# Moving the low parts of split weights 64 bytes off the grid of the other operands

## Chip, cores and metric

The kernel runs on one core of a Trainium2 chip. The time is in device microseconds for one execution; lower is better.

## What is computed

Two layers of a hybrid block on 256 tokens of width 1024, all in float32. Each layer has a SwiGLU feed-forward network, a mixer (a gated short convolution, a gated linear recurrence and a multi-scale pooling side by side), cross-attention to a memory of 256 tokens, and a second SwiGLU network, each followed by a layer norm:

```python
def reference(x, mem, ...):
    h = x
    for l in range(DEPTH):                                   # DEPTH = 2
        h = layer_norm(ALPHA * h + 0.5 * swiglu(h, ffn1_gate[l], ffn1_up[l], ffn1_down[l]), ...)
        z = h @ w_in[l]
        cb, cc, ch, rq, rf, ri, rg, pu = jnp.split(z, split_at, axis=-1)
        y_conv = short_gated_conv(ch, cb, cc, conv_w[l])
        y_rec = hgrn2(rq, rf, ri, rg, lbs[l], rec_norm_g[l])
        y_pool = multiscale_pool(pu, pool_w[l], pool_scale[l])
        mix = jnp.concatenate([y_conv, y_rec, y_pool], axis=-1) @ w_out[l]
        h = layer_norm(ALPHA * h + mix, ...)
        h = layer_norm(ALPHA * h + cross_attn(h, mem, ca_q[l], ca_k[l], ca_v[l], ca_o[l]), ...)
        h = layer_norm(ALPHA * h + 0.5 * swiglu(h, ffn2_gate[l], ffn2_up[l], ffn2_down[l]), ...)
    return h
```

Nearly all the work is in the products with the weights (1024 x 2816, 1024 x 1024 and the like), which are read once from HBM.

## The kernel before

Every large product is made in three passes of the type float32r. Each operand is split into a high part, its value rounded to float32r, and a low part, the rest. The product is then high x high + high x low + low x high. Weights come in slabs: `load` (line 62) issues a DMA of 1 MB into a tile `raw` of 128 partitions x 2048, and splits it in halves of 128 x 1024. `split` (line 58) is two instructions: ScalarE copies `raw` to `whi` (line 59), and VectorE subtracts that from `raw` into `wlo` (line 60). `raw` has 3 buffers, `whi` and `wlo` have 8 each. The activations are kept transposed and split as well: `xT` (and `mT` for the memory) holds for each of 8 blocks of 128 channels 256 columns of high parts and, right behind them, 256 of low parts.

Two helpers make the products:

- `mm_cols` (line 94) makes 128 output columns for all tokens. The weight block is the stationary operand. Seven products of the high part with 512 columns of `x`, high and low side by side (line 97), eight of the low part with the 256 high columns (line 99), and the last of the high part (line 100).
- `mm_rows` (line 108) makes 512 output columns for 128 tokens. The activation is stationary and the weights stream past it: line 109 high by high, line 110 the low weights, line 111 the low activations with the high weights.

TensorE's weight load of a matmul is a record of its own in the profile (PEld) and runs beside the matmul before it. The order of the work is the order of the program on each engine's queue; the tile framework places the waits, from the tiles and their numbers of buffers.

What the change is about is where tiles lie in SBUF. Each partition has its memory filled pool after pool, in the order in which the pools are opened, and in a pool tag after tag. The framework's constants and the small tiles `prm`, `invc`, `lbs`, `oml` and `nhalf` (padded to 16 columns) fill the first 512 bytes, so that all that follows begins on a multiple of 512: `h`, the unit matrices, `xT`, `mT`, `kTh`, `kTl`, `rows`, `wpool` and `masks` (896 bytes used of a tile of 1024) in the pool `cst`; then `raw`, `whi`, `wlo` and the layer norm's `lng` and `lnb` in the pool `wp`; then the pool `sm` of small statistics, and behind it the pools of the stages (`ffn`, `mix`, `att`), which share one place. In the mixer's pool some tiles at the end don't begin on such a multiple: `cv`, `win` and `u` begin 320 bytes past one. `masks` holds, as bytes, which pairs of positions belong to each of 7 levels of the recurrence. GpSimd makes it once (line 201), and line 597 reads it in slices of 64 bytes.

Of the kernel before, what the change touches and what calls it, by code (L numbers as in the profile page):

```python
# [8 lines left out]
F32 = mybir.dt.float32  # L9
F32R = mybir.dt.float32r  # L10
U8 = mybir.dt.uint8
# [6 lines left out]
P = 128  # L18
DEPTH = 2
SEQ = 256  # L20
DM = 1024
DFF = 2816
NT = SEQ // P
# [6 lines left out]
LEVELS = (1, 2, 4, 8, 16, 32, 64)  # L30
# [16 lines left out]
def model(ctx: ExitStack, tc: tile.TileContext, t: dict, out: bass.AP):  # L47
    nc = tc.nc
    cst = ctx.enter_context(tc.tile_pool(name="cst", bufs=1))
    wp = ctx.enter_context(tc.tile_pool(name="wp", bufs=1))  # L50
    sm = ctx.enter_context(tc.tile_pool(name="sm", bufs=2))
    ps = ctx.enter_context(tc.tile_pool(name="ps", bufs=4, space=PSUM))

# [4 lines left out]
    def split(hi, lo, src):  # L58
        nc.scalar.copy(hi, src)  # L59
        nc.vector.tensor_tensor(lo, src, hi.bitcast(F32), op=ALU.subtract)  # L60

    def load(src, k0, nk, c0, ncol, fine=False):


        hi, lo, todo = [], [], []
        step = 2048 // ncol
        for a in range(k0, k0 + nk, step):
            raw = wp.tile([P, 2048], F32, tag="raw", name="raw", bufs=3)
            raw = raw.rearrange("p (k c) -> p k c", c=ncol)
            half = step // 2  # L70
            part = 1 if fine else step
            for b in range(0, step, part):
                nc.sync.dma_start(
                    raw[:, b : b + part, :],
                    src[(a + b) * P : (a + b + part) * P, c0 : c0 + ncol].rearrange("(k p) c -> p k c", p=P),
                )
            for s in range(2):
                h = wp.tile([P, 1024], F32R, tag="whi", name="whi", bufs=8)
                w = wp.tile([P, 1024], F32R, tag="wlo", name="wlo", bufs=8)
                h = h.rearrange("p (k c) -> p k c", c=ncol)  # L80
                w = w.rearrange("p (k c) -> p k c", c=ncol)
                r = raw[:, s * half : (s + 1) * half, :]
                if fine:
                    todo += [(h[:, b, :], w[:, b, :], r[:, b, :]) for b in range(half)]
                else:
                    split(h, w, r)
                hi.append(h)
                lo.append(w)
        return Weights(hi, lo, half, todo)
# [23 lines left out]
    def tok(i):  # L113
        return slice(i * P, (i + 1) * P)
# [6 lines left out]
    oml = cst.tile([P, DEPTH, HEADS], F32, name="oml")  # L121
    nhalf = cst.tile([P, 16], F32, name="nhalf")[:, 0:HEADS]
    h = [cst.tile([P, DM], F32, name=f"h{i}") for i in range(NT)]
    for i in range(NT):
        for n in range(2):
            c = slice(n * 512, n * 512 + 512)
            nc.sync.dma_start(h[i][:, c], t["x"][0, tok(i), c])
# [24 lines left out]
    def load_memory(mp):  # L152
# [10 lines left out]

    rows = cst.tile([P, P], F32, name="rows")
    wpool = cst.tile([P, DEPTH, 2, P], F32, name="wpool")
    masks = cst.tile([P, 1024], U8, name="masks")[:, 0 : NT * len(LEVELS) * 64].rearrange(
        "p (b n c) -> p b n c", b=NT, c=64
    )
    nc.gpsimd.memset(nhalf, -0.5)
    cw = prm[:, 0:12].rearrange("p (l k j) -> p l k j", l=DEPTH, j=2)  # L170
    ng = prm[:, 20:28].rearrange("p (l h) -> p l h", l=DEPTH)
# [66 lines left out]


    def ln_params(l, n):  # L240
        g = wp.tile([P, DM], F32, tag="lng", name="lng")
        b = wp.tile([P, DM], F32, tag="lnb", name="lnb")
        nc.sync.dma_start(g, t["ln_g"][l, n : n + 1, :].to_broadcast([P, DM]))
        nc.sync.dma_start(b, t["ln_b"][l, n : n + 1, :].to_broadcast([P, DM]))
        return g, b
# [83 lines left out]
    def ffn(l, name, n, pend=None, last=False, early=None):  # L329
        gate, up, down = (t[f"{name}_{x}"][l] for x in ("gate", "up", "down"))  # L330
        with tc.tile_pool(name="ffn", bufs=2, reuse_waits="tile") as fp:
# [7 lines left out]
            def first():  # L339

                ah, al = act_tiles()
                wg = load(gate, 0, NK, 0, CHUNK, fine=pend is None)
                wu = load(up, 0, NK, 0, CHUNK) if pend is not None else None

                def products(o, w, i, k):
# [15 lines left out]
                if pend is None:  # L361
# [5 lines left out]
                    with tc.manual_schedule(engines={E.Activation, E.DVE, E.PE}):  # L367
# [5 lines left out]
                        for a in range(0, NK, 2):  # L373
                            for k in range(a + 4, min(a + 6, NK)):
                                split(*wg.todo[k])
                            group(0, wg, a)
                    wu = load(up, 0, NK, 0, CHUNK)
                    for a in range(0, NK, 2):
                        group(1, wu, a)
# [64 lines left out]
            for c, (c0, ncol) in enumerate(chunks):  # L444
                if c:
                    acts.append(hidden(c0, ncol, late))
                    late = None
                else:
                    a, late = first()
                    acts.append(a)  # L450
                    ys = [[acc((P, 512), "dn") for _ in range(2)] for _ in range(NT)]
                if c == 1:
                    gb = ln_params(l, n)
                if c == 1 and early is not None:
                    rest = early(fp)
                if c == 2 and early is not None:
                    for f in rest:
                        f()
                if c > 0:
                    if c > 1:  # L460
                        both(c - 2, 1)
                    if c < len(chunks) - 1:
                        both(c - 1, 0)
# [38 lines left out]
    def mixer(l, fill):  # L502
        w_in = t["w_in"][l]
        with tc.tile_pool(name="mix", bufs=1, reuse_waits="tile") as mp:
# [31 lines left out]
            columns(1280, 512, lambda j, o: add(f[:, :, j, :], o, by_tile), ev_f)  # L536
            columns(768, 512, lambda j, o: add(q[:, :, j, :], o, by_tile))
            gb = ln_params(l, 1)
            w = load(w_in, 0, NK, 1792, 512)
            for i in range(NT):  # L540
# [171 lines left out]
    def attention(l, pend):  # L712
        scale = (DM // HEADS) ** -0.5
        with tc.tile_pool(name="att", bufs=1, reuse_waits="tile") as ap:
# [62 lines left out]
            values(l, 0, vh, vl, {6: pend})  # L777
            query(0)
            gb = ln_params(l, 2)
            query(1, lambda: (weights(0), weights(1)))  # L780
            values(
# [48 lines left out]
```

## Time and profile before

| | |
|---|---|
| median of 3 runs | 1174.87 us (1174.75 to 1176.64) |
| the profiled execution | 1176.58 us, of it 1174.8 us span of instructions |
| granted TensorE clock | 0.998 |
| TensorE busy, matmuls | 1161.9 us (99%) |
| TensorE busy, weight loads | 1001.2 us (85%) |
| VectorE busy | 824.7 us (70%) |
| ScalarE busy | 595.6 us (51%) |
| DMA | 218.23 MB, 186 GB/s on average |

A busy share is the part of the span in which the engine had an instruction under way. For matmuls it counts overlapping ones once, and their ends are modelled, so starts are the better guide to their pace. "PE" is the matmuls, "PEld" the weight loads, DVE is VectorE, ACT is ScalarE. The chain that ended last is followed back from the last instruction, at each step to what released it.

### The profile page before, as it was taken

How to read it: one execution, taken by the hardware profiler on the slowest of the kernel's cores; microseconds unless marked ns; L12 is line 12 of the kernel's file. 1: busy time of each engine (PE TensorE's matmuls, PEld its weight loads, DVE VectorE, ACT ScalarE, POOL GpSimd, SP SyncE). 2: the span in 40 equal slices, each digit the busy share in tenths (PEclk: the TensorE clock that was granted, in tenths of full speed). 3: DMA queues.
4: the chain of work that ended last, by engine and by line, in shares of the span. 5: the costliest groups of instructions: out<-in, count | busy, mean ns of one | idle time of the engine just before them, and what ended most of it. 6: DMA issues, size and time to landing. Idle time of an engine off the chain costs nothing.

```text
span 1174.8 us, 15745 instructions
## 1 busy us (share of the span) xinstructions
PE 1161.9 (99%) x6219; PEld 1001.2 (85%) x6219; DVE 824.7 (70%) x1194; ACT 595.6 (51%) x873; POOL 40.1 (3%) x80
## 2 busy tenths in 40 slices
PE   8999999999999999999999999999999999999997
PEld 6888888888889888888888888888888888888886
DVE  5766567889787666566677665687998777665665
ACT  6555553626456355455355555446354653554550
POOL 7000000000000000000000000000000000000000
PEclk9999999999999999999999999999999999999999
DMA  8655564644474375655466544655255545655440
GB/s 327 252 193 201 174 221 143 220 140 151 172 244 167 96 247 180 215 198 196 144 215 221 202 168 169 228 187 194 73 209 183 212 144 177 217 179 203 164 171 36
DMA packets 98522, 218.23 MB, mean 186 GB/s; under 512 B 3792, under 2 KB 16368, under 8 KB 98448
## 3 DMA queue, kind: packets, MB, share of 16 engines
q1 hardware_dynamic: 97968, 216.68, 53.2%
q8 instruction: 49, 0.80, 0.3%
q10 hardware_dynamic: 288, 0.39, 0.1%
q14 instruction: 25, 0.20, 0.0%
q0 software_dynamic: 192, 0.15, 0.0%
HBM read 216.15 MB, written 1.05 MB: 185 GB/s over the span
## 4 chain that ended last, share of the span: by engine, by line
PE 97%; DVE 2%; DMA 0%; ACT 0%; issue 0%; SPq 0%; DVEq 0%; ACTq 0%
PE acc L97 29%; PE acc L99 17%; PE dn L111 10%; PE dn L109 10%; PE dn L110 9%; PE acc L109 5%; PE acc L110 5%; PE acc L111 5%; PE acc L100 4%; PE acc L149 1%; PE dn L578 1%; DMA raw<-in_ffn_gate_dram 0%; DVE wlo L60 0%; DVE AT L597 0%; PE dn L621 0%; PE acc L759 0%
## 5 line engine op out<-in xcount | busy, mean ns | idle before, releaser
L60 DVE TENSOR_TENSOR wlo<-raw,whi 128x1024 fp32r<-128x1024 f32 (+1 forms) x396 | 471.1, 1209 | 129.7 <-ACT whi L59 73.6
L59 ACT CAST whi<-raw 128x1024 fp32r<-128x1024 f32 (+1 forms) x396 | 399.7, 1043 | 208.2 <-PE dn L111 140.9
L97 PE MATMUL acc<-xT,whi 128*128 128x512 f32 x1400 | 358.5, 393 | 0.0
L97 PEld LDWEIGHTS acc<-xT,whi 128*128 128x128 f32 x1400 | 262.2, 188 | 50.3
L99 PEld LDWEIGHTS acc<-xT,wlo 128*128 128x128 f32 x1600 | 218.3, 190 | 15.5
L99 PE MATMUL acc<-xT,wlo 128*128 128x256 f32 x1600 | 223.5, 282 | 0.0
L109 PE MATMUL dn<-whi,ah 128*128 128x512 f32 x346 | 135.3, 391 | 0.0
L111 PE MATMUL dn<-whi,al 128*128 128x512 f32 x346 | 134.8, 389 | 0.0
L110 PE MATMUL dn<-wlo,ah 128*128 128x512 f32 x346 | 134.6, 389 | 0.0
L105 DVE TENSOR_TENSOR sg<-acc,sg 128x256 f32<-128x256 f32 x72 | 30.4, 422 | 78.4 <-ACT sg L104 78.4
L100 PE MATMUL acc<-xT,whi 128*128 128x512 f32 x200 | 79.2, 396 | 0.0
L111 PEld LDWEIGHTS dn<-whi,al 128*128 128x128 f32 x346 | 64.9, 188 | 13.7
L110 PEld LDWEIGHTS dn<-wlo,ah 128*128 128x128 f32 x346 | 65.0, 188 | 13.5
L109 PEld LDWEIGHTS dn<-whi,ah 128*128 128x128 f32 x346 | 65.1, 188 | 12.6
L104 ACT COPY sg<-acc 128x256 f32<-128x256 f32 x72 | 26.6, 370 | 94.7 <-PE acc L100 94.7
L109 PE MATMUL acc<-whi,xT 128*128 128x512 f32 x160 | 63.4, 397 | 0.1
L110 PE MATMUL acc<-wlo,xT 128*128 128x512 f32 x160 | 63.0, 393 | 0.0
L111 PE MATMUL acc<-whi,xT 128*128 128x512 f32 x160 | 62.8, 392 | 0.0
L104 ACT COPY up<-acc 128x256 f32<-128x256 f32 x72 | 26.6, 370 | 59.8 <-PE acc L100 59.8
L105 DVE TENSOR_TENSOR up<-acc,up 128x256 f32<-128x256 f32 x72 | 30.3, 421 | 31.8 <-ACT up L104 31.8
L109 PE MATMUL dn<-whi,xT 128*128 128x512 f32 x128 | 50.3, 393 | 0.0
L111 PE MATMUL dn<-whi,xT 128*128 128x512 f32 x128 | 49.9, 390 | 0.0
(202 smaller groups left out, 1236.9 us busy)
## 6 DMA issues: line engine op xcount, KB each, us to landing
raw<-in_ffn_up_dram SPq DMA_DIRECT2D x44, 1024.0 KB, 5.0
raw<-in_ffn_down_dram SPq DMA_DIRECT2D x44, 1024.0 KB, 4.8
raw<-in_ffn_gate_dram SPq DMA_DIRECT2D x42, 1024.0 KB, 5.0
raw<-in_w_in_dram SPq DMA_DIRECT2D x24, 1024.0 KB, 5.0
raw<-in_ca_k_dram SPq DMA_DIRECT2D x8, 1024.0 KB, 4.9
raw<-in_w_out_dram SPq DMA_DIRECT2D x8, 1024.0 KB, 4.8
raw<-in_ca_v_dram SPq DMA_DIRECT2D x8, 1024.0 KB, 5.6
raw<-in_ca_q_dram SPq DMA_DIRECT2D x8, 1024.0 KB, 4.9
```

What stands on the lines that cost most here:

```text
L59: nc.scalar.copy(hi, src)
L60: nc.vector.tensor_tensor(lo, src, hi.bitcast(F32), op=ALU.subtract)
L97: nc.tensor.matmul(o, w.at(k, cols)[0], x[:, k], start=k == 0, stop=False)
L99: nc.tensor.matmul(o[:, 0, :], w.at(k, cols)[1], x[:, k, 0, :], start=False, stop=False)
L100: nc.tensor.matmul(o, w.at(NK - 1, cols)[0], x[:, NK - 1], start=False, stop=True)
L104: nc.scalar.copy(dst, view(o[:, 1, :]))
L105: nc.vector.tensor_tensor(dst, view(o[:, 0, :]), dst, op=ALU.add)
L109: nc.tensor.matmul(o, xh, wh, start=start, stop=False)
L110: nc.tensor.matmul(o, xh, wl, start=False, stop=False)
L111: nc.tensor.matmul(o, xl, wh, start=False, stop=stop)
L149: nc.tensor.transpose(pt[:, k, :], src[:, (4 * j + k) * P : (4 * j + k + 1) * P], unit)
L578: nc.tensor.matmul(o[:, hh], kc[:, hh, :], view(qf, hh * P + c, (other - c, 2), (2 * c, a), (1, c)), start=True, stop=True,)
```

## The change

A pool `off` with one unused tile of 64 bytes is opened behind `wp`, then a pool `wl` that holds the eight buffers of `wlo`, then a pool `wr`. In `wr` lie `masks`, without its padding, an unused tile of 64 bytes, and `lng` and `lnb`. So `wlo` begins 64 bytes past a multiple of 512, `masks` as well, and `lng`, `lnb` and all behind them lie on multiples of 512 again. The computation and the order of the instructions are the same.

```diff
@@ model
     cst = ctx.enter_context(tc.tile_pool(name="cst", bufs=1))
     wp = ctx.enter_context(tc.tile_pool(name="wp", bufs=1))
+
+    off = ctx.enter_context(tc.tile_pool(name="off", bufs=1))
+    wl_ = ctx.enter_context(tc.tile_pool(name="wl", bufs=1))
+    wr = ctx.enter_context(tc.tile_pool(name="wr", bufs=1))
     sm = ctx.enter_context(tc.tile_pool(name="sm", bufs=2))
@@ load
                 h = wp.tile([P, 1024], F32R, tag="whi", name="whi", bufs=8)
-                w = wp.tile([P, 1024], F32R, tag="wlo", name="wlo", bufs=8)
+                w = wl_.tile([P, 1024], F32R, tag="wlo", name="wlo", bufs=8)
@@ model
     h = [cst.tile([P, DM], F32, name=f"h{i}") for i in range(NT)]
+    off.tile([P, 16], F32, name="skip")
+    masks = wr.tile([P, NT * len(LEVELS) * 64], U8, name="masks").rearrange("p (b n c) -> p b n c", b=NT, c=64)
+    wr.tile([P, 16], F32, name="fill")
     for i in range(NT):
@@ model
     wpool = cst.tile([P, DEPTH, 2, P], F32, name="wpool")
-    masks = cst.tile([P, 1024], U8, name="masks")[:, 0 : NT * len(LEVELS) * 64].rearrange(
-        "p (b n c) -> p b n c", b=NT, c=64
-    )
     nc.gpsimd.memset(nhalf, -0.5)
@@ ln_params
-        g = wp.tile([P, DM], F32, tag="lng", name="lng")
-        b = wp.tile([P, DM], F32, tag="lnb", name="lnb")
+        g = wr.tile([P, DM], F32, tag="lng", name="lng")
+        b = wr.tile([P, DM], F32, tag="lnb", name="lnb")
```

## The prediction

> **What bounds the kernel now.** I read the page first: busy shares, then the chain that ended last.
>
> ```profile
> span 1174.8 us, 15745 instructions
> ...
> PE 1161.9 (99%) x6219; PEld 1001.2 (85%) x6219; DVE 824.7 (70%) x1194; ACT 595.6 (51%) x873; POOL 40.1 (3%) x80
> ...
> PE 97%; DVE 2%; DMA 0%; ACT 0%; issue 0%; SPq 0%; DVEq 0%; ACTq 0%
> ```
>
> TensorE is the bound nearly everywhere: 97% of the chain is matmuls. So a change pays or costs only by what it does to the distance from one matmul to the next, times their number. The grouped instructions say which matmuls read the low parts (wlo), and who writes them.
>
> ```profile
> L60 DVE TENSOR_TENSOR wlo<-raw,whi 128x1024 fp32r<-128x1024 f32 x388 | 465.9, 1219 | 127.3 <-ACT whi L59 71.3 <-PE acc L99 49.0
> ...
> L99 PE MATMUL acc<-xT,wlo 128*128 128x256 f32 x1600 | 223.5, 282 | 0.0
> L99 PEld LDWEIGHTS acc<-xT,wlo 128*128 128x128 f32 x1600 | 218.3, 190 | 15.5
> ...
> L110 PE MATMUL dn<-wlo,ah 128*128 128x512 f32 x346 | 134.6, 389 | 0.0
> ...
> L110 PE MATMUL acc<-wlo,xT 128*128 128x512 f32 x160 | 63.0, 393 | 0.0
> ...
> L110 PE MATMUL dn<-wlo,xT 128*128 128x512 f32 x128 | 49.8, 389 | 0.0
> ...
> L110 PE MATMUL acc<-wlo,mT 128*128 128x512 f32 x64 | 24.9, 390 | 0.0
> ...
> L99 PE MATMUL acc<-mT,wlo 128*128 128x256 f32 x128 | 17.8, 282 | 0.0
> ```
>
> The code gives the roles. In mm_cols (line 99) the low part is the stationary operand, which PEld loads while the matmul before it streams x: 1600 + 128 = 1728 times. In mm_rows (line 110) it is the moving operand: 346 + 160 + 128 + 64 = 698 times; twelve short ones in the tail are left out. So 1728 + 698 = 2426 matmuls now find one operand 64 bytes off where the other, read at the same time, is on a multiple of 512. The mean durations (282, 389) are not the cost, because matmuls overlap; the cost is from start to start, which the timeline shows.
>
> ```profile
> 300.21 1.12 PE L99 MATMUL acc<-mT,wlo 128*128 128x256 f32 x8
> ...
> 301.17 0.40 PE L100 MATMUL acc<-mT,whi 128*128 128x512 f32 x1
> ...
> 301.40 0.40 PE L109 MATMUL dn<-whi,xT 128*128 128x512 f32 x1
> ...
> 301.64 0.39 PE L110 MATMUL dn<-wlo,xT 128*128 128x512 f32 x1
> ...
> 302.56 0.39 PE L111 MATMUL dn<-whi,xT 128*128 128x512 f32 x1
> ...
> 303.24 0.39 PE L111 MATMUL dn<-whi,xT 128*128 128x512 f32 x1
> ```
>
> Eight matmuls of 256 columns fill 301.17 - 300.21 = 0.96 us, 120 ns each. Three of 512 columns fill 303.24 - 302.56 = 0.68 us, 226.7 each. The difference, 106.7 for 256 columns, is streaming; so each matmul, long or short, carries 120 - 106.7 = 13.3 ns besides. That is all an address could remove, and the first thing it could make longer. The reader should also see that the distance isn't fixed: the run begins at 301.40 with a step of 0.24 us, and its five steps to 302.56 take 1.16 us, 232 each, before it settles at 226.7. Something between load and stream depends on how the two stand to each other in time.
>
> **The change part by part.** No instruction is added, removed or reordered: the two fillers are never written, the masks are only declared earlier, and every DMA, wait and queue stays in its order. The three new pools hold tiles of the same numbers of buffers, so the same reuse of buffers sets the same waits. The 64 + 896 + 64 bytes of skip, masks and fill are the 1024 that the masks took, so lng, lnb and all that follows keep their addresses; raw and whi move by a whole 1024. Left are four things that an address could touch.
>
> *VectorE writing wlo.* 388 long instructions of 1219 ns. For other writes at odd places there are rows: with tiles of the same form, sg lies on a multiple of 512, cv 320 bytes past one, u's columns 328 past one.
>
> ```profile
> L637 DVE TENSOR_TENSOR sg<-acc,half 128x128 f32<-128x128 f32 x8 | 2.3, 283 | 0.0
> ...
> L637 DVE TENSOR_TENSOR cv<-acc,half 128x128 f32<-128x128 f32 x8 | 2.2, 280 | 0.0
> ...
> L637 DVE TENSOR_TENSOR u<-acc,half 128x128 f32<-128x128 f32 x4 | 1.1, 282 | 0.0
> ```
>
> 283, 280, 282: nothing to see, at most 1%. Of 1219 that would be 12 ns, 388 x 12 = 4.7 us of VectorE, which is idle 30% of the span and 2% of the chain; hidden but for 2% of that, 0.1 us. If the cover were gone (VectorE the bound) it would be 4.7 us either way. I take 0.
>
> *The masks.* They now begin 64 bytes later; 28 instructions read them in slices that began at multiples of 64 before too.
>
> ```profile
> L597 DVE COPY_PREDICATED AT<-masks,dn x28: 423/438/810, 249.0 to 844.3; 128x256 f32<-128x256 uint8 x28
> ```
>
> 28 x 0.438 = 12 us in all; 1% of it, either sign, is 0.1 us, and VectorE's slack hides it. I take 0.
>
> *wlo as stationary operand* (1728) and *as moving operand* (698). No row of the trace shows a matmul of this type with one operand 64 off. The nearest are the mixer's plain f32 products: line 621 has both operands on multiples of 512; line 578 at its levels 16, 32 and 64 begins the first half of its moving operand 64, 128 and 256 bytes off, the second half on a multiple (the last three groups of that line in a layer); line 680 streams win, 320 off, past weights on a multiple.
>
> ```profile
> 258.31 1.05 PE L578 MATMUL dn<-q,kc 128*128 128x128 f32 x8
> ...
> 261.31 1.06 PE L578 MATMUL dn<-q,kc 128*128 128x128 f32 x8
> ...
> 264.32 1.05 PE L578 MATMUL dn<-q,kc 128*128 128x128 f32 x8
> ...
> 267.19 1.06 PE L621 MATMUL dn<-v,AT 128*128 128x128 f32 x8
> ...
> 277.33 1.02 PE L680 MATMUL acc<-win,wpool 128*128 128x256 f32 x4
> ...
> L578 PE MATMUL dn<-q,kc x112: 270/275/377, 247.2 to 843.0; 128*128 128x128 f32 x112
> ...
> L680 PE MATMUL acc<-win,wpool x8: 377/378/379, 277.3 to 855.9; 128*128 128x256 f32 x8
> ```
>
> Line 621, aligned: (1.06 - 0.275)/7 = 112 ns apart. Line 578 at 64, 128, 256 bytes off: (1.05 - 0.275)/7 = 111, 112 and 111. So between operands that differ by just the offset of this change, and operands that don't, there is at most 1 ns. That is the row nearest to the question, and I take its value: 0 for both roles. Its weakness: these products stream at half the rate (line 680 needs (1.02 - 0.38)/3 = 213 ns for 256 columns, where line 99 needs 120), so a stall could hide in slack that the fast ones lack.
>
> The bounds. Below: line 680, with its moving operand off the multiples, streams for as long as a 512-column product and has 213 where that has 226.7. If the shift brought this to all 698 moving uses, 698 x 13.3 = 9.3 us; and if the 1728 loads came down from 120 to line 621's 112, 1728 x 8 = 13.8 us: together -23 us. Above: the step of 0.24 us at 301.40 against 0.2267, 13.3 ns more; on all 2426, +32 us. The milder mean of those five steps, 232, is 5.3 ns more: +13 us.
>
> On the same 226.7 ns, the Trainium skill (TensorE: Matmul & The Clock Gate, "Back-to-back issue gap") gives an isolated gap of columns / 2.4 + 2.5 ns, 216 for 512 columns. This case's matmuls don't agree (226.7), line 680's 213 nearly does; by the page's figure as an estimate, moving uses alone would gain 698 x 11 = 7.7 us.
>
> The sum: 0 + 0 + 0 + 0. The profiled execution took 1176.58 us (1174.8 of span and 1.8 around it) and stays there; the runs shown have a median of 1174.87, 1.7 below it. I forecast 1175.0 as median.
>
> Why the nearest row may also hold for fast streams: over one load the matmul reads twice as fast as the load. Whatever residue of 512 bytes the two begin at, the faster sweeps past the slower once through all of them; an offset moves the moment of meeting, not the number of meetings. That is argued, not shown.
>
> **The rivals.**
>
> *Faster: load and stream stop meeting.* The 13.3 ns are the price of both operands starting at the same residue at nearly the same time; 64 bytes apart they miss each other. For it: the same 13.3 ns at both lengths, as if something happened once a load; line 680's 213; the unsettled 232. Against it: line 578 shows no gain over line 621. Full price 1174.9 - 23 = 1152; if half is recovered, 1163. The gain may also come in one role and be lost in the other, which leaves the larger number, the 1728 loads, in charge.
>
> *Slower: the low parts' operands stall.* Place: each load of wlo beside a stream of x, and each stream of wlo beside a load of x. Off the multiple, either takes more pieces or keeps the pair in the unsettled state that the trace shows after line 100. Price 5.3 ns x 2426 = 13 us, 1188; at most 32 us, 1207. It decides from 1 ns a matmul on (2426 x 1 = 2.4 us, the bound of what is measurable). For it: 232 and 240 do occur in aligned operands, so the loss isn't at its maximum; nothing shows that the aligned state is not the best. Against: lines 578 and 680.
>
> *Slower by VectorE.* If the subtraction of line 60 lost 10%, 122 ns, its 388 would take 47 us more; VectorE would be busy (825 + 47)/1175 = 74%, and late only where it already is: in the head, where the first weights are split.
>
> ```profile
> 10.00:35.00 25.00, 25.00 (x108) 20.63 (x109) 18.25 (x24) 17.32 (x23) 11.47 (x25) 1.00 0.96 359
> ```
>
> There VectorE has 18.25 of 25 us; some 15 long subtractions x 0.12 = 2 us, perhaps 4 with the other stages' beginnings: 1179. It decides from about 7% on. Against it: 280 to 283 ns above.
>
> *It doesn't do what it says:* a pool that begins on its own rounded address would swallow the 64 bytes. Then 1175, inside my forecast. The Trainium skill (SBUF — State Buffer, "Who interferes with whom") would have the same result for another reason, since PE has separate read ports for loads and stream and waits on nobody; no run here shows the two ports apart.
>
> **How the numbers follow.** What a measurement of this kernel can tell from no change is about 0.2%, 2.4 us. No change: 0.34 (lines 578 and 621 speak for it, but on half-rate products only). Faster: 0.32. Slower by TensorE: 0.28; slower by VectorE: 0.06; together 0.34. Sides are nearly even, because the sign of an effect on the fast products is not in the trace. The likeliest case alone has 1172.5 to 1177.5. For 8 in 10 the range takes of the faster case all but its last quarter (down to -17 us) and of the slower one up to +21: 1158 to 1196.
>
> **What would show it.** Right: line 99 still 120 ns, line 110 and its neighbours 226.7 from start to start, line 60 at 1219, PE at 1162 busy. The faster rival: eight of line 99 in less than 0.94 us, or the step after line 109 below 220. The slower: more than 0.97 us for the eight, or steps in mm_rows that stay at 232 or above. VectorE's: line 60 above 1300, and idle TensorE ended by wlo. My forecast is wrong if any of these distances moves by over 1 ns, whatever the rest does.

## The result, and the profile after

The changed kernel is slower by 0.7%: a median of 1183.50 us (1183.23 to 1184.48, 6 runs) against 1175.55 us (1174.56 to 1176.71, 6 runs) for the kernel before; the ratio is 1.0069, with a 95% interval of 1.0056 to 1.0082. The profiled execution has a span of 1182.8 us, 8.0 more than before.

The page of the kernel after: the span, the busy times, and the chain that ended last by engine.

```profile
span 1182.8 us, 15745 instructions
...
PE 1169.7 (99%) x6219; PEld 998.3 (84%) x6219; DVE 825.5 (70%) x1194; ACT 596.1 (50%) x873; POOL 40.0 (3%) x80
...
PE 97%; DVE 2%; DMA 1%; ACT 0%; issue 0%; SPq 0%; DVEq 0%; ACTq 0%
```

The number of instructions is the same, and TensorE is still the bound. Its busy time grew by 7.8 us, which is nearly the whole difference; VectorE and ScalarE have what they had. The granted clock was 0.999, against 0.998 before. (Lines are shifted: 97, 99, 100 are now 101, 103, 104; 109 to 111 are 113 to 115; 60 is 64.) The groups say the same of VectorE, which writes the moved tile:

```profile
L64 DVE TENSOR_TENSOR wlo<-raw,whi 128x1024 fp32r<-128x1024 f32 x388 | 465.8, 1219 | 131.7 <-ACT whi L63 81.5 <-PE acc L103 49.0
```

1219 ns, as before. So the difference lies in the distances between matmuls. The timeline of the same stretch that the prediction showed, one block of mm_cols and the mm_rows behind it:

```profile
302.03 1.11 PE L103 MATMUL acc<-mT,wlo 128*128 128x256 f32 x8
302.97 0.39 PE L104 MATMUL acc<-mT,whi 128*128 128x512 f32 x1
303.20 0.40 PE L113 MATMUL dn<-whi,xT 128*128 128x512 f32 x1
303.44 0.39 PE L114 MATMUL dn<-wlo,xT 128*128 128x512 f32 x1
303.67 0.39 PE L115 MATMUL dn<-whi,xT 128*128 128x512 f32 x1
303.90 0.40 PE L113 MATMUL dn<-whi,xT 128*128 128x512 f32 x1
...
306.68 0.40 PE L113 MATMUL dn<-whi,xT 128*128 128x512 f32 x1
```

Eight of line 103 take 302.97 - 302.03 = 0.94 us, 117.5 each, where they took 120: with the low part as stationary operand the kernel got faster. The fifteen steps from 303.20 to 306.68 take 3.48 us, 232 each. Before, they stumbled at 232 for five steps and then settled at 226.7, in a pattern of 226, 227 and 227 ns that repeats for as long as the run of matmuls lasts. Now they never reach that pace, and all three lines are slow: 232 ns on average each, also 113 and 115, whose own operands still lie on multiples of 512. Taken in nanoseconds from the trace, the starts show that the slow pace isn't a stumble that goes on: it repeats too, after fifteen steps of 225 to 240 ns that add up to 3.48 us.

For the whole kernel I took the distance from each matmul's start to the next in the traces, leaving out those over 300 ns, and averaged them by role; the runs' first steps, before the pace repeats, are in these means. Four roles: the 512-column products of mm_cols, its 256-column ones (the stationary low part), and mm_rows on the feed-forward's `ah` and `al`, and on `xT` and `mT`. Their numbers are 1695, 1728, about 1033 and about 1036 in every kernel.

| kernel | ratio to before (95%) | mm_cols 512, ns | mm_cols 256, ns | mm_rows ah/al, ns | mm_rows xT/mT, ns | span, us |
|---|---|---|---|---|---|---|
| before | 1 | 230.0 | 119.1 | 227.2 | 227.4 | 1174.8 |
| after (wlo 64 off) | 1.0069 (1.0056 to 1.0082) | 230.0 | 117.7 | 232.1 | 232.0 | 1182.8 |
| ctl0 | 1.0003 (0.9994 to 1.0013) | 230.0 | 119.1 | 227.2 | 227.3 | 1174.4 |
| all64 | 1.0003 (0.9994 to 1.0013) | 230.0 | 119.1 | 227.2 | 227.4 | 1174.8 |
| hilo64 | 1.0011 (1.0002 to 1.0021) | 232.7 | 114.5 | 229.4 | 230.0 | 1176.6 |
| al64 | 1.0069 (1.0054 to 1.0084) | 229.9 | 117.7 | 232.3 | 232.0 | 1183.4 |
| lo32 | 1.0069 (1.0054 to 1.0084) | 230.8 | 118.4 | 231.8 | 231.9 | 1183.7 |
| lo128 | 1.0120 (1.0103 to 1.0137) | 230.7 | 120.3 | 233.3 | 232.6 | 1189.9 |
| lo256 | 0.9997 (0.9988 to 1.0006) | 230.0 | 119.1 | 227.2 | 227.3 | 1174.7 |
| lo448 | 1.0042 (1.0028 to 1.0057) | 232.4 | 117.9 | 229.2 | 229.3 | 1181.0 |
| x192 | 0.9991 (0.9982 to 1.0001) | 232.7 | 114.3 | 227.6 | 229.2 | 1172.6 |
| x128 | 1.0076 (1.0062 to 1.0090) | 232.7 | 118.5 | 227.3 | 232.4 | 1183.4 |
| x64 | 1.0006 (0.9996 to 1.0015) | 229.5 | 116.0 | 227.8 | 233.4 | 1175.4 |
| x224 | 1.0090 (1.0073 to 1.0107) | 232.9 | 118.9 | 226.8 | 233.3 | 1186.7 |

The sum for the kernel after: 1728 x (117.7 - 119.1) = -2.4 us, 1033 x 4.9 = +5.1 and 1036 x 4.6 = +4.8: +7.5 of the 8.0 us. So the change is one gain and one loss four times as large, both on TensorE.

### The profile page after: what moved, and what is told of

Read it like the earlier page. It is cut to its first block, busy times and chain, and to the rows that moved or that the text cites. A ratio compares the mean times of both kernels' runs of the same rounds, so it can differ in the third digit from the quotient of the medians.

```text
span 1182.8 us, 15745 instructions
## 1 busy us (share of the span) xinstructions
PE 1169.7 (99%) x6219; PEld 998.3 (84%) x6219; DVE 825.5 (70%) x1194; ACT 596.1 (50%) x873; POOL 40.0 (3%) x80
## 4 chain that ended last, share of the span: by engine, by line
PE 97%; DVE 2%; DMA 1%; ACT 0%; issue 0%; SPq 0%; DVEq 0%; ACTq 0%
PE acc L101 29%; PE acc L103 17%; PE dn L113 10%; PE dn L115 10%; PE dn L114 10%; PE acc L113 5%; PE acc L114 5%; PE acc L115 5%; PE acc L104 4%; PE acc L156 1%; PE dn L582 1%; DMA raw<-in_ffn_gate_dram 1%; DVE wlo L64 0%; DVE AT L601 0%; PE dn L625 0%; PE acc L362 0%
```

## The experiments

**Is it the 64 bytes?** ctl0 keeps the new pools and the moved masks, but not the skip, so that wlo lies on multiples of 512 again.

```diff
-    off.tile([P, 16], F32, name="skip")
...
-    wr.tile([P, 16], F32, name="fill")
+    wr.tile([P, 32], F32, name="fill")
```

> The new pools and the moved masks alone: the skip of 64 bytes is gone, wlo lies on multiples of 512 again. All theories that put the loss on the 64 bytes expect the time of before (within 0.2%), line 103 at 120 ns from start to start and lines 113 to 115 at 226.7. If the pools or the masks cost anything, it stays near 1183.

1176.41 us against 1176.13, ratio 1.0003, and every distance as before. So the pools cost nothing. ctl0 puts the masks back on a multiple of 512 too, but the kernel after reads them at the median of before, 438 ns:

```profile
L601 DVE COPY_PREDICATED AT<-masks,dn x28: 423/438/797, 251.0 to 850.1; 128x256 f32<-128x256 uint8 x28
```

With 7.5 of the 8.0 us found in the matmuls that read wlo and their neighbours, the 64 bytes of wlo are the cause.

**The place itself, or its distance from the others?** all64 is the kernel before with one number changed: everything behind `nhalf` moves by 64 bytes, all operands together.

```diff
-    nhalf = cst.tile([P, 16], F32, name="nhalf")[:, 0:HEADS]
+    nhalf = cst.tile([P, 32], F32, name="nhalf")[:, 0:HEADS]
```

> Every large operand lies 64 bytes off the multiples of 512, so no two differ (made from the kernel before, with nhalf padded by 64 bytes more). Theory R (only the distance between the operand that streams and the one that is loaded beside it counts): the time of before, 226.7 and 120 ns. Rival A (an operand off the multiple costs by itself): worse than after, since all of lines 97 to 111 are off: all three lines of mm_rows at 232 or more and mm_cols changed too, 1183 or above.

Ratio 1.0003. The timeline of all64 in the same stretch:

```profile
300.15 1.12 PE L99 MATMUL acc<-mT,wlo 128*128 128x256 f32 x8
301.11 0.40 PE L100 MATMUL acc<-mT,whi 128*128 128x512 f32 x1
...
302.49 0.39 PE L111 MATMUL dn<-whi,xT 128*128 128x512 f32 x1
...
303.85 0.39 PE L111 MATMUL dn<-whi,xT 128*128 128x512 f32 x1
```

0.96 us for eight, and 1.36 us for six steps, 226.7 each: the settled pace. Nothing is lost by lying off the multiples of 512; rival A falls. What counts is how the operands lie to each other.

**Both parts of the weights off.** hilo64 moves whi beside wlo, 64 bytes off; the activations stay.

```diff
-                h = wp.tile([P, 1024], F32R, tag="whi", name="whi", bufs=8)
+                h = wl_.tile([P, 1024], F32R, tag="whi", name="whi", bufs=8)
```

> High and low parts of the weights both 64 bytes off, activations on the multiples. Theory R: in mm_rows every stream is now 64 off the load beside it, not one in three, so its pace is at least as bad as the 232 ns of after (1183 or more, if mm_cols' long products don't gain). Rival M (the loss comes from the change of distance between one matmul and the next, 0, 64, 0): mm_rows has one distance throughout and settles at 226.7 again, while line 103 keeps its 118: 1172. Rival A: as R, worse than after.

Ratio 1.0011. Its timeline:

```profile
300.48 1.07 PE L103 MATMUL acc<-mT,wlo 128*128 128x256 f32 x8
301.39 0.39 PE L104 MATMUL acc<-mT,whi 128*128 128x512 f32 x1
...
302.55 0.39 PE L114 MATMUL dn<-wlo,xT 128*128 128x512 f32 x1
...
305.98 0.39 PE L114 MATMUL dn<-wlo,xT 128*128 128x512 f32 x1
```

Eight of line 103 need 0.91 us, 114 each, 6 less than before. mm_rows needs 3.43 us for fifteen steps, 229: better than 232, and not 226.7. This pace repeats as well, in the feed-forward mostly as 226, 229, 232. So neither theory had its numbers. R is wrong that three off-streams of three are as bad as one of three; M is wrong that one distance throughout settles at 226.7. By the table, the short products of mm_cols gain 1728 x 4.6 = 7.9 us, its long ones lose 1695 x 2.7 = 4.6 and mm_rows about 5.0: a little slower in all.

**Bringing the pairs back to distance 0.** al64 is the kernel after with the feed-forward's low activations 64 bytes off too.

```diff
                 ah = fp.tile([P, 4, SEQ], F32R, tag="ah", name="ah", bufs=3)
+                if not acts:
+                    fp.tile([P, 16], F32, name="askip", bufs=1)
                 al = fp.tile([P, 4, SEQ], F32R, tag="al", name="al", bufs=3)
+                if not acts:
+                    fp.tile([P, 112], F32, name="afill", bufs=1)
```

> As after, and the feed-forward's low activations (al) 64 bytes off as well. Line 114 then streams wlo (64) while al (64) is loaded, line 113 streams whi (0) while ah (0) is loaded: every pair read at the same time is at distance 0. Theory R: mm_rows of the feed-forward (346 triples) goes back to 226.7, the other 352 stay at 232: about 346 x 3 x 5.3 = 5.5 us less than after, 1178. Rival A: one more operand off, no better than after. Rival M, if it is the streamed operand's own change of place that counts: as after, 1183.5.

1.0069, just as after. The feed-forward's mm_rows in its timeline:

```profile
179.27 0.40 PE L113 MATMUL dn<-whi,ah 128*128 128x512 f32 x1
...
182.06 0.40 PE L113 MATMUL dn<-whi,ah 128*128 128x512 f32 x1
```

2.79 us for twelve steps, 232.5. Making each stream agree with the load that the profile shows beside it isn't enough. R in that form falls: something else counts as well. A stream's own load and the stream before it are candidates: in lines 114 and 115 of al64 each stream lies 64 bytes off its own load, one way and the other, and the place of the stream changes from line to line. These runs don't settle which.

**At which distances?** Four kernels move wlo by other amounts; in lo32 and lo128 only the sizes of skip and fill differ from the kernel after (lo128 has no fill), in lo256 and lo448 part of the masks serves as the skip. The diff is cut to the lines that set the distance; its comments say which kernel has which.

```diff
-    off.tile([P, 16], F32, name="skip")
+    off.tile([P, 8], F32, name="skip")           # lo32; 32 columns in lo128
...
+    mk = [(off, wr)[b].tile([P, len(LEVELS) * 64], U8, name=f"masks{b}") for b in range(NT)]   # lo448
...
+    mk = [(off, wr)[g].tile([P, NT * (2, len(LEVELS) - 2)[g] * 64], U8, name=f"masks{g}") for g in range(2)]   # lo256
```

> wlo 32 bytes off instead of 64, all else as after. If the settled pace needs the same place modulo 128 bytes (theory P128), this is another unsettled case: mm_rows not at 226.7, a time that is neither that of before nor exactly that of after, 1177 to 1190. If any 64-byte piece counts as one place (P64), it is the time of before.

1.0069, mm_rows at 231.8: a distance of 32 bytes already changes the pace. P64 falls.

> wlo 128 bytes off. P128 (32 columns of the stream, which take the 13.3 ns that each matmul carries, are 128 bytes): mm_rows at 226.7 and line 103 at 120 again, the time of before within 0.2%. P512 (only multiples of 512 are alike): as after or otherwise slower, 1180 or more.

1.0120, the slowest kernel of the study. Fifteen steps of mm_rows in its timeline:

```profile
306.32 0.40 PE L113 MATMUL dn<-whi,xT 128*128 128x512 f32 x1
...
309.82 0.40 PE L113 MATMUL dn<-whi,xT 128*128 128x512 f32 x1
```

3.50 us, 233.3 a step, and the short products of mm_cols lose their gain (120.3 in the table). P128 falls.

> wlo 256 bytes off; the masks are split in two tiles, two levels ahead of wlo and five behind, so that all the rest keeps its place. P128 and a theory of 256: the time of before. P512: 1180 or more.

0.9997. Six steps in its timeline:

```profile
302.50 0.39 PE L115 MATMUL dn<-whi,xT 128*128 128x512 f32 x1
...
303.86 0.39 PE L115 MATMUL dn<-whi,xT 128*128 128x512 f32 x1
```

1.36 us, 226.7 each. 256 bytes off is as good as 0, in all four roles: P512 falls too. So the place seems to count modulo 256 bytes; that rests on this distance and on one more pair of kernels below.

> wlo 448 bytes off, which is 64 modulo 128; the masks of the first token tile lie ahead of it, those of the second behind. P128: the pattern of after to the nanosecond (mm_rows 232, line 103 at 118), 1183.5. If the sign or the size of the distance counts (the load ahead of the stream or behind it), another pattern and time.

1.0042, another pattern than after's: mm_rows at 229.2, mm_cols' long products at 232.4. 448 is 192 modulo 256, so by that reading wlo lies 64 bytes short of the others' places instead of 64 past them, and the sign of the distance counts.

**Moving the activations instead.** If only the difference modulo 256 counts, xT and mT at 192 must give mm_cols what both weights at 64 gave it, while the feed-forward's mm_rows, on ah and al, stays aligned. The kernels x192, x128, x64 and x224 are the kernel before with the lines below; the comments give the sizes in the other three.

```diff
+    cst.tile([P, 48], F32, name="xskip")         # x192; 32 in x128, 16 in x64, 56 in x224
     xT = cst.tile([P, NK, 2, SEQ], F32R, name="xT")
     mT = cst.tile([P, NK, 2, SEQ], F32R, name="mT")
+    cst.tile([P, 16], F32, name="xfill")         # x192; 32, 48, 8
```

> Made from the kernel before: the weights stay, and xT and mT lie 192 bytes past a multiple of 256, so that weights and activations in mm_cols differ by 64 modulo 256 as when both parts of the weights were 64 off. If only the difference modulo 256 counts: mm_cols as there (eight of line 99 in 0.91 us, a block of sixteen in 2.773 us for 2.793, 216 x -0.02 = -4.3 us), mm_rows on xT and mT at 228.9 as there (352 triples x 3 x 2.2 = +2.3 us), the feed-forward's mm_rows on ah and al at 226.7 as before: 2.0 us less than before, 0.998. If it is the weights' own place, the time of before.

The timeline of x192, first the feed-forward's mm_rows, then the block of mm_cols and the mm_rows on xT:

```profile
179.03 0.39 PE L111 MATMUL dn<-whi,al 128*128 128x512 f32 x1
...
182.43 0.39 PE L111 MATMUL dn<-whi,al 128*128 128x512 f32 x1
...
298.63 1.07 PE L99 MATMUL acc<-mT,wlo 128*128 128x256 f32 x8
299.55 0.39 PE L100 MATMUL acc<-mT,whi 128*128 128x512 f32 x1
...
300.93 0.39 PE L111 MATMUL dn<-whi,xT 128*128 128x512 f32 x1
...
304.37 0.39 PE L111 MATMUL dn<-whi,xT 128*128 128x512 f32 x1
```

The feed-forward: 3.40 us for fifteen steps, 226.7. Line 99: 0.92 us for eight, 115. mm_rows on xT: 3.44 us for fifteen, 229.3. All three paces are within about 1 ns of the expected ones, and the table has hilo64 and x192 within 0.2 ns in mm_cols and 0.8 in mm_rows on xT: it is the difference that counts, modulo 256, whichever side is moved. The time is less clear. By the table the gain is 1.3 us for the 2.0 expected, the medians differ by 1.0 us, and the ratio is 0.9991 with an interval of 0.9982 to 1.0001, which still touches 1. So x192 is faster than the kernel after, and no gain over the kernel before is shown.

> xT and mT 128 bytes off, weights on the multiples. By the theory of the difference modulo 256 some other pace for mm_cols (no row to work it out from), mm_rows of the feed-forward at 226.7; every pair of xT with a weight has the same distance, so less spread than with the low parts alone 128 off (1.012): 0.995 to 1.010.

1.0076; the feed-forward's mm_rows at 227.3, on xT at 232.4. Within the expected band, and less than lo128.

> xT and mT 64 bytes off: the opposite sign of distance from x192. If the sign doesn't count, the same pace and 0.998; if it does, another: 0.995 to 1.008. Feed-forward mm_rows at 226.7 in any case.

1.0006: the short products gain 3.1 ns, mm_rows on xT loses 6.0.

```profile
302.03 0.39 PE L109 MATMUL dn<-whi,xT 128*128 128x512 f32 x1
...
305.53 0.39 PE L109 MATMUL dn<-whi,xT 128*128 128x512 f32 x1
```

These are 3.50 us for fifteen steps, 233.3 each, where x192 has 229.3. The opposite sign gives another pace in every role that it touches.

> xT and mT 224 past a multiple of 256, so weights and activations in mm_cols differ by 32: between the distances 0 (2.793 us for a block of sixteen) and 64 (2.773). If the pace changes evenly with the distance: about 2.783, 216 x -0.01 = -2.2 us, mm_rows on xT at 227.8, +1.2 us; 0.999. If it is a matter of particular places, another time on either side, as 32 bytes did for the low parts alone (1.007). A version that beats the kernel before would need less than 0.998.

1.0090. A distance of 32 bytes between all weights and activations does not lie between 0 and 64: the short products are at 118.9 and the long ones at 232.9. The pace isn't a smooth function of the distance. No version that clearly beats the kernel before came out of these runs.

## Why the prediction was right and wrong

The forecast, no change, was wrong, also by the prediction's own sign: the distances moved by 2.5 and 5.3 ns, and 1 was the limit. The measured 1183.5 us lies in the range because the range was made to take in the rivals; what came is nearest to the rival "slower: the low parts' operands stall", which had 0.28.

- **The bound and what could change.** TensorE's steps, and nothing else: right. Line 60 stayed at 1219 ns, the masks' reading at a median of 438, ctl0 shows the pools to be free.
- **The step that failed** is the choice of the nearest row for the two roles of wlo. Line 578 and line 621 differ by 64 bytes and both need 111 to 112 ns; I took their difference, at most 1 ns, for that of the fast products. The weakness was written beside it: those products stream at half the rate. The fast ones lose 4.6 to 4.9 ns a step in mm_rows and gain 1.4 in mm_cols. A row at another rate was no evidence against a stall. Why the slow products show nothing stays open.
- **The argument behind it**, that a stream sweeps past every place of the load once, whatever the offset, and so meets it equally often, falls with x128 and x224: a constant distance does change the pace of mm_rows on xT, to 232 and 233. It was labelled as argued.
- **The slower rival** gave two reasons. "Off the multiple, either takes more pieces" falls with all64. The other, that it "keeps the pair in the unsettled state", is nearer: the pace of before is indeed not reached. But what came instead is a repeating pattern of its own, and that its mean is the 232 ns of the five steps at 301.40 is luck as far as these runs show, since other distances end at 229 to 233. The upper bound was too high: the step of 0.24 us is 236 ns in the trace, 9.3 more than 226.7 and not 13.3. The count was wrong in two ways. It charged 5.3 ns to 2426 uses, among them the 1728 loads, which in fact gained; and it left out lines 109 and 111, which are slowed along with 110. With 3 x 698 = 2094 steps at 5.3 ns, less the 2.4 us gained, the sum would have been 8.7 us; 8.0 were measured. The two errors have opposite signs, so that the rival's 13 us is not far off is partly luck.
- **The faster rival** named the 1728 loads as the place where a gain could be, with 8 ns from line 621. There was a gain, of 1.4 ns after this change and up to 4.8 in x192. It also said that a gain in one role and a loss in the other would leave the 1728 loads in charge; it was the other way round, because each of the 698 streams slows two neighbours as well. Line 680's 213 ns was never reached by a fast product: the lowest repeating pace of mm_rows in any run is 226.7.
- **VectorE** as a bound: nothing of it in the profile.
- **The Trainium skill** (SBUF — State Buffer, "Who interferes with whom") gives PE separate ports for loads and stream, and says that PE waits on nobody. The prediction took from it that the offset would change nothing; the section says nothing of places. In these runs they matter: the same mm_rows took from 226.8 to 233.4 ns a step on average with nothing changed but where the operands lie. Through which port or wait, no run shows.

## What to carry to other kernels

Where float32r matmuls with a new stationary operand each follow one another without a pause, give all their operands the same place modulo 256 bytes, and pad the small tiles ahead of them to keep it. In this kernel that was worth up to 1.2%, and none of the other placements tried was clearly better. A shift that looks like a gain in one role of a tile must be summed over all its roles, and over the neighbours in the same run of matmuls, since here a single odd operand in three slowed all three. When the only similar rows in a trace run at another rate, they bound nothing. Look instead at whether the pace in the trace is fixed or stumbles: a stumble among aligned operands showed here that the pace can change.

## What the hardware showed that I had not expected

- In a long run of mm_rows TensorE's pace falls into a repeating pattern, which depends on the operands' places. With all places alike it is 226, 227, 227 ns, mean 226.7, found again within two to ten steps after each disturbance. In the kernel after it is fifteen steps of 224 to 241, mean 232.0; in lo448 steps of 228 to 230, mean 229; on xT in x64 steps of 230 to 236, mean 233.3. So a misplaced operand is seen in the mean pace, and not always in uneven steps. What makes a pattern no run shows; the instructions and their order were the same in all these kernels but for the masks' in lo256 and lo448.
- The distance has a sign: weights 64 bytes past the activations' place modulo 256 (x192) give 114.3 ns for the short products of mm_cols and 229.2 in mm_rows; 64 short of it (x64) they give 116.0 and 233.4.
- Not settled: which pairs must agree. al64 gives every stream the place of the load that the profile shows beside it, and stays at 232. The stream before it alone doesn't explain the rest: in hilo64 and in mm_rows on xT of x192, x128, x64 and x224 every stream has the place of the one before, and the pace still changes. A stream's own load is off wherever the pace changed, but no run moved it alone. A kernel with the low parts off in mm_cols alone wasn't tried.
